# High weights against high and low moving parts: two 256-column matmuls into the same columns, in two of three pairs of retention's heads

## The chip, the cores and the metric

The kernel runs on one core of a Trainium2 chip. The metric is the device time of one execution in microseconds (us). Five engines work side by side, each with its own instruction row: TensorE (PE; PEld are its weight loads), VectorE (DVE), ScalarE (ACT), GpSimd (POOL) and SyncE (SP). They wait for one another through semaphores.

## The reference, cut to what matters

One layer of a streaming encoder on 512 frames of width 2048, in float32. The part that matters here is the large projection and retention:

```python
h = rmsnorm(x, norm_gain)
proj = h @ w_in                                  # 2048 x 13392
(aq, ak, av, az, iq, ik, iw, rq, rk, rv, rz, ga, gb) = jnp.split(proj, SPLIT_POINTS, axis=-1)
...
rq = rope(rq.reshape(B, L, R_HEADS, R_KEY_DIM), positions)
rk = rope(rk.reshape(B, L, R_HEADS, R_KEY_DIM), positions) * (R_KEY_DIM ** -0.5)
b_out = retention_mixer(rq, rk, rv, ret_gn_gain) * jax.nn.silu(rz)
merged = jax.nn.sigmoid(ga) * (a_out @ w_a_out) + jax.nn.sigmoid(gb) * (b_out @ w_b_out)
```

Eight retention heads need a query and a key block of 128 channels each; the gates `ga` and `gb` have 16 blocks each.

## The kernel before

**Precision by parts.** A float32 product is made of float16 parts. A weight block is split into `wh` (high, cast by ACT at L257) and `wl` (the rest, by DVE at L143), the moving operand likewise. Three of the four part products are kept: `wh` times high, `wh` times low and `wl` times high.

**Pairs of blocks.** `gemm_pair` (L361) computes two output blocks of 128 channels for 512 frames at once from seven products instead of eight (Strassen-Winograd form). Its moving operands (`hs`, `ha` in the profile) are sums of quarters of the normed input; each has 256 columns of high parts and 256 of low parts side by side, `LO` and `HI`. A product is a run of 8 matmuls of `wh` with all 512 columns (L435) and a run of 8 of `wl` with the 256 high columns. So after it a PSUM bank's left half holds high terms and its right half the `wh` times low terms, and the two halves are still to be added. Four banks `v`, `p`, `q`, `r` serve the seven products, in the order v, p, q, r, p, v, p; some products are added onto what a bank holds already.

**Taking out.** After certain products ACT copies a bank to SBUF (`copy`, L371: tiles `pv` and `e`). `out` (L375) takes the sum or difference of a bank and such a copy into `e_t`, 512 wide, and `done` (L1484) adds the two halves of `e_t` into a quarter of the output tile `go`. Each pair does this four times: after the third product from `q`, after the sixth from `v`, and after the seventh from `p` and then from `r`. When a 512-column output has both its quarters, `finish` follows: for gates ACT's sigmoid (L1493) and a store, for retention's pair the rotation (L1174 on ACT, L1179 to L1181 on DVE).

**Weights.** Raw blocks come by SP's queue; some are summed with another block by POOL's accumulating DMA (L221) once the first `wl` of them is made, some by DVE (L268). `wh` and `wl` have three slots each. `e`, `pv` and `e_t` are among the tiles that share 28 slots (`U`).

**Order.** Instructions stand in each engine's row as the code is called; nothing reorders them. Work beside the matmuls is put off by a count of steps (`later(n, f)`), and a step is counted in `gemm_pair` after every two values of `k`, so each deferred instruction falls at a set place among TensorE's matmuls.

**The place.** The stage from 248 to 720 us runs eight heads. Each has three pairs: retention's query and key (`u_r[h]`, whose `finish` starts that head's retention) and two gate pairs (`u_g[2h]`, `u_g[2h+1]`). Retention's own steps (splits, scores, states, norm) are spread over the following two pairs and the next head's first. Rounds of a top-k (L1074, L1077) stand among them on DVE. The next stages run four `rz` pairs and eight attention pairs in the same way. Late in the kernel two stages run `gemm_pair` with `turned`, in which a `wh` already takes high and low parts as two matmuls of 256 columns into the same columns, for some of its products.

A second, general program of the same block follows in the code for inputs that the float16 one can't serve; it is not run here.

Of the kernel before, what the change touches and what calls it, by code (L numbers as in the profile page):

```python
# [16 lines left out]
AF = mybir.ActivationFunctionType  # L17
# [20 lines left out]
class General:  # L38


    fast = False
# [7 lines left out]
class Fast:  # L49


    fast = True
    dt = F16
    w = 2.0 ** 13
    x = 2.0 ** 4
# [17 lines left out]
def block_kernel(tc, flag, cfg, xT, pT, posb, posq, w_in, w_v, w_r0, w_r1, w_ik, w_a, w_b, w_o, w_ple, w_gate,  # L73
                 w_gt, w_pt, fgb, tab, gains, cst, dec, out, out_a, out_b):
    nc = tc.nc
    pe, dve, act, pool, sp = nc.tensor, nc.vector, nc.scalar, nc.gpsimd, nc.sync

    fast = cfg.fast
    un_x, un_a, un_m, un_r, un_p = (1.0 / (cfg.w * v) for v in (cfg.x, cfg.a, cfg.m, cfg.r, cfg.p))

    with contextlib.ExitStack() as ctx:
# [11 lines left out]
        def U(name, dt=F32):  # L93
            return up.tile([128, L], dt, name=name, tag="u")
# [250 lines left out]
        ALL = slice(0, L)  # L345
# [5 lines left out]
        LO, HI = slice(0, 256), slice(256, 512)  # L351
# [6 lines left out]
        SPLIT_AT = {0: 3, 2: 4, 3: 4, 4: 5, 7: 6, 8: 7, 10: 8, 12: 9}  # L358
        LOAD_AT = (0, 2, 4, 6, 8, 10, 12)

        def gemm_pair(ids, X, done, late=False, turned=False, nk=8, more=None):  # L361

            p, v, q, r = (P("ps_" + n) for n in ("p", "v", "q", "r"))
            E = {}

            def copy(n, src):
                E[n] = U(n)  # L370
                act.activation(E[n], src, AF.Copy)  # L371

            def out(f, x, y, i, c):
                t = U("e_t")
                f(t, x, y)  # L375
                done(t[:, LO], t[:, HI], i, c)

            def minus_both(t, x, y):
                dve.scalar_tensor_tensor(t, x, -1.0, y, op0=OP.mult, op1=OP.subtract)

            add, sub = dve.tensor_add, dve.tensor_sub
            f_q, f_pv, f_r = (add, minus_both, sub) if turned else (sub, sub, add)

            def last():
                copy("e3", p)
                out(f_pv, p, E["pv"], 1, HI)
                out(f_r, r, E["e3"], 1, LO)

            def first():
                if turned:  # L390
                    E["e1"] = U("e1")
                    act.activation(E["e1"][:, LO], p[:, LO], AF.Copy)
                else:
                    copy("e1", p)

            def second():
                if turned:
                    done(q[:, LO], E["e1"][:, LO], 0, LO)
                else:
                    out(f_q, q, E["e1"], 0, LO)  # L400

            after = {
                0: lambda: copy("pv", v),
                1: first,
                2: second,
                4: lambda: copy("e2", p),
                5: lambda: out(f_q, v, E["e2"], 0, HI),
                6: last,
            }
            banks = (v, p, q, r, p, v, p)  # L410
            runs = [(n, part, range(nk)) for n, part in RUNS]
            early = 4
            if late:
                runs[0:early] = [(n, part, ks) for ks in (range(7), (7,)) for n, part, _ in runs[0:early]]
            ended = [0] * 7
            count = 0
            for at, (n, part, ks) in enumerate(runs):
                at = max(at - early, 0) if late else at
                i, o = ids[n], banks[n]
                if more is not None:  # L420
                    more(at)
                elif at in SPLIT_AT and not (late and at == 2):
                    split_to(ids[0] + SPLIT_AT[at], (1 if state["turn"] else 5) if at == 2 else 1)
                if at in LOAD_AT and more is None:
                    load_to(ids[LOAD_AT.index(at)] + AHEAD + LOADS)
                if waiting and state["banks"] and 4 <= at <= 9:
                    bias_banks(waiting.popleft())
                w, c = loaded[i][part], (ALL, LO)[part]
                begin = ended[n] == 0
                for k in ks:  # L430
                    ended[n] += 1
                    x = X[PRODUCTS[n]][k]
                    moving = [(LO, v) for v in x[:2 - part]] if turned and isinstance(x, tuple) else [(c, x[:, c])]
                    for j, (co, src) in enumerate(moving):
                        pe.matmul(o[:, co], w[:, k], src, start=(n < 4 and begin and k == 0 and j == 0),  # L435
                                  stop=(ended[n] == 2 * nk), skip_group_check=True)
                    count += 1
                    if count % (16 // nk) == 0:
                        step()
                if ended[n] == 2 * nk and n in after:  # L440
                    after[n]()
# [168 lines left out]
        u_r, u_g = [], []  # L610
        for h in range(NH):
            u_r.append(block_pair(col(RQ, h), col(RK, h)))
            for n in (2 * h, 2 * h + 1):
                g, m = ((GB, 2 * n), (GA, 2 * n - 16))[n >= 8]
# [9 lines left out]
        for n in range(1, 16):  # L624
            for at in NARROW_AT if fast else ():
                if at // 8 == n - 1:
                    for _, f in list(to_make)[:LOOK]:
                        f[0]()
                    m, f = to_make.popleft()
# [42 lines left out]
        cs = cp.tile([128, 130], F32, name="cs")  # L672
# [313 lines left out]
        Xh, h_step = combos(lambda k: xn[k], lambda k: xn[k + 8], "h", lambda n, k: x_at.get((n, k)))  # L986
# [99 lines left out]
        for r in range(16):  # L1086
            for t in range(1, NT):
                f = lambda r=r, t=t: topk_round(t, r == 15)
# [382 lines left out]
            if late_rounds:  # L1471
                late_rounds.popleft()()

        def gate_pair(ids, finish):
            if state["banks"]:
                for n in ROUNDS_AT:
                    later(n, late_round)
            t = B("go")
            outs = [t[:, 0:512], t[:, 512:1024]]
            have = [0, 0]  # L1480

            def done(c0, c1, i, q):
                o = outs[i]
                dve.tensor_add(o[:, q], c0, c1)  # L1484
                have[i] += 1
                if have[i] == 2:
                    later(1, lambda: finish(i, o))

            gemm_pair(ids, Xh, done)

        def to(dst, func):
            def finish(i, o):
                act.activation(o, o, func, scale=un_x)  # L1493
                later(2 if fast else 0, lambda: act.dma_start(dst[i], o))
            return finish
# [5 lines left out]
        for h in range(NH):  # L1501
            if fast and h == NH - 1:
                state["rate"] = BG_RATES[3]
            if state["rate"] == BG_RATES[2]:
                later(38, lambda: hold(True))
                later(64, lambda: hold(False))
            if fast:
                for n in ROUNDS_IN_HEAD if h else ():
                    later(n, late_round)
            gate_pair(u_r[h], retention(h))  # L1510
            for n in (2 * h, 2 * h + 1):
                d, m = ((sgb, 2 * n), (sga, 2 * n - 16))[n >= 8]
                state["turn"] = fast and n == 2 * h
                gate_pair(u_g[n], to(d[m:m + 2], AF.Sigmoid))
        state["rate"] = BG_RATES[4]
        state["banks"] = True
        for n, u in enumerate(u_rz):
            y = B("y2")
# [232 lines left out]
        for m in PAIRED:  # L1751
# [19 lines left out]
            elif m - 8 not in narrow:  # L1771
                t = B("sm")
                s, o = t[:, 0:512], t[:, 512:1024]
# [64 lines left out]
        for m in range(MF):  # L1838
            i = u_p[m // 4][0]
# [3 lines left out]
            h, l = loaded[i]  # L1843
# [324 lines left out]
        if fast:  # L2168
# [36 lines left out]
RET_SPLITS = {("k", 0): 16, ("k", 1): 21, ("q", 0): 18, ("q", 1): 24, ("v", 0): 26, ("v", 1): 37,  # L2205
              ("vd", 0): 40, ("vd", 1): 45}
KEYS_AT = 30, 31
ROUNDS_AT = 19, 44
ROUNDS_IN_HEAD = 15, 44, 106, 106
QK_LOW = 5, 9  # L2210
# [105 lines left out]
```

## Time and profile before

| | us |
|---|---|
| median of 3 runs | 1551.54 (1551.16 to 1551.79) |
| the profiled execution | 1552.11 |
| its span, first to last instruction | 1550.3 |
| retention's heads in it | 248.4 to 720 |

The granted clock of TensorE is 0.998 of full speed over the span. In the profile's rows the first number is the start in us from the span's start, the second the duration; a row such as `ps_r<-hs,wh 128*128 128x512 f16 x8` is eight matmuls into bank `ps_r` with `hs` moving and `wh` loaded, 512 columns each. What stands in brackets is the idle time just before, and what ended it. Matmuls are pipelined: a run's modelled end lies later than the next run's possible start. Rows of groups give durations in ns as least, median and greatest.

### The profile page before, as it was taken

Reading aid. Unit: us, or ns where it says so; the run is one execution under the profiler, and the core shown is the slowest. Engines: PE = TensorE matmul, PEld = TensorE weight load, DVE = VectorE, ACT = ScalarE, POOL = GpSimd, SP = SyncE. Lnnn points to the kernel's source line nnn. Section 1 sums busy time; section 2 is a strip of 40 time slices with the busy share of each in tenths; the row PEclk is TensorE's granted clock in tenths of the full one; section 3 lists DMA queues with packets and bytes.
Section 4 is the critical chain, followed back from the end, with each engine's and each line's share of the span. In section 5 each row is a group of like instructions: output and inputs, shape, how many; then the busy total and the mean of one; then the engine's idle time right before and its main releaser. Section 6 shows DMA issues by size and latency. Waiting matters only on the chain.

```text
span 1550.3 us, 26188 instructions
## 1 busy us (share of the span) xinstructions
PE 1532.5 (99%) x9537; PEld 896.5 (58%) x9537; DVE 1357.5 (88%) x2776; ACT 978.1 (63%) x1491; POOL 224.4 (14%) x261
## 2 busy tenths in 40 slices
PE   9999999999999999999999999999999999999997
PEld 5654445666656656556555665655555556647765
DVE  8899889999999999998788888788879999998975
ACT  7565545665665665687877776577633555576654
POOL 3000121111111111112441121200000111101101
PEclk9999999999999999999999999999999999999999
DMA  8436989899898899789999999999666899878974
GB/s 323 133 120 204 259 215 248 217 226 233 211 229 230 207 231 232 205 221 258 287 251 242 225 249 232 262 357 345 208 211 190 204 224 234 236 225 233 264 213 148
DMA packets 136269, 358.15 MB, mean 231 GB/s; under 512 B 22209, under 2 KB 34753, under 8 KB 136129
## 3 DMA queue, kind: packets, MB, share of 16 engines
q1 hardware_dynamic: 94368, 230.08, 43.8%
q0 software_dynamic: 28656, 101.20, 34.9%
q10 hardware_dynamic: 13104, 25.09, 4.4%
q8 instruction: 76, 1.25, 0.3%
q14 instruction: 65, 0.52, 0.1%
HBM read 311.76 MB, written 42.99 MB: 229 GB/s over the span
## 4 chain that ended last, share of the span: by engine, by line
PE 65%; DVE 20%; ACT 7%; issue 4%; DMA 3%; ACTq 0%; SPq 0%; DVEq 0%
PE ps_p L435 18%; PE ps_v L435 12%; PE ps_r L435 6%; DVE wl L143 6%; PE ps_q L435 5%; DVE e_t L375 3%; ACT wh L257 2%; PE ps_vn L1142 2%; PE ps_vn L1144 2%; PE ps_vn L1143 2%; PE ps_iq L337 1%; PE ps_iq L339 1%; PE ps_iq L338 1%; DVE go L1484 1%; DVE wraw L268 1%
## 5 line engine op out<-in xcount | busy, mean ns | idle before, releaser
L143 DVE SCALAR_TENSOR_TENSOR wl<-wraw,wh 128x1024 f16<-128x1024 f32 (+3 forms) x461 | 557.0, 1220 | 90.6 <-ACT wh L257 89.4
L257 ACT ACTIVATE wh<-wraw 128x1024 f16<-128x1024 f32 (+3 forms) x484 | 489.2, 1024 | 131.7 <-DVE wraw L268 75.9
L435 PEld LDWEIGHTS <-wh 128*128 128x128 f16 x3224 | 313.5, 98 | 317.9 <-ACT wh L257 9.9
L435 PEld LDWEIGHTS <-wl 128*128 128x128 f16 x2968 | 287.8, 98 | 72.8 <-DVE wl L143 9.6
L221 POOL DMA_DIRECT2D wraw<-w_in x120 | 106.6, 972 | 564.4 <-DVE wl L143 482.2
L435 PE MATMUL ps_p<-hs,wh 128*128 128x512 f16 x640 | 152.5, 379 | 0.0
L371 ACT ACTIVATE e<-ps_p 128x512 f32<-128x512 f32 x158 | 93.0, 589 | 51.3 <-PE ps_p L435 42.0
L435 PE MATMUL ps_p<-hs,wl 128*128 128x256 f16 x640 | 84.4, 273 | 1.6 <-ACT rq L1190 1.1
L435 PE MATMUL ps_r<-hs,wh 128*128 128x512 f16 x320 | 75.7, 379 | 2.5 <-ACT wh L257 2.2
L435 PE MATMUL ps_q<-ha,wh 128*128 128x512 f16 x320 | 75.7, 379 | 0.0
L435 PE MATMUL ps_v<-ha,wh 128*128 128x512 f16 x320 | 75.6, 379 | 0.0
L435 PE MATMUL ps_v<-hs,wh 128*128 128x512 f16 x320 | 75.6, 379 | 0.0
L435 PE MATMUL ps_p<-ha,wh 128*128 128x512 f16 x320 | 75.6, 379 | 0.0
L1493 ACT ACTIVATE go<-go 128x512 f32<-128x512 f32 x40 | 25.2, 630 | 79.1 <-DVE go L1484 79.1
L1484 DVE TENSOR_TENSOR go<-e_t 128x256 f32<-128x256 f32 x160 | 68.0, 425 | 5.8
L1037 ACT ACTIVATE mk<-relf,thr 128x512 f16<-128x512 f32 (+3 forms) x128 | 67.5, 553 | 1.3 <-ACT go L1493 1.2
L268 DVE TENSOR_TENSOR wraw<-wraw 128x1024 f32<-128x1024 f32 x53 | 64.9, 1225 | 1.8
L339 PEld LDWEIGHTS <-wl 128*128 128x128 f16 x396 | 38.8, 98 | 40.2 <-DVE wl L143 0.2
L337 PEld LDWEIGHTS <-wh 128*128 128x128 f16 x396 | 38.9, 98 | 37.0 <-DVE z L150 0.3
L338 PEld LDWEIGHTS <-wh 128*128 128x128 f16 x396 | 38.8, 98 | 36.5
L221 POOL DMA_DIRECT2D wraw<-w_o x24 | 21.1, 932 | 235.7 <-DVE wl L143 101.3
L339 PE MATMUL ps_w<-bh,wl 128*128 128x512 f16 x128 | 48.5, 379 | 0.0
(467 smaller groups left out, 2885.3 us busy)
## 6 DMA issues: line engine op xcount, KB each, us to landing
wraw<-w_in SPq DMA_DIRECT2D x170, 512.0 KB, 5.6
wraw<-w_in POOLq DMA_DIRECT2D x120, 512.0 KB, 8.1
wraw<-w_o SPq DMA_DIRECT2D x32, 512.0 KB, 5.6
wraw<-w_o POOLq DMA_DIRECT2D x24, 512.0 KB, 7.6
wraw<-w_gate SPq DMA_DIRECT2D x24, 512.0 KB, 5.3
wraw<-w_v SPq DMA_DIRECT2D x16, 512.0 KB, 7.7
wraw<-w_b SPq DMA_DIRECT2D x16, 512.0 KB, 6.5
wraw<-w_gate POOLq DMA_DIRECT2D x15, 512.0 KB, 7.2
```

What stands on the lines that cost most here:

```text
L143: dve.scalar_tensor_tensor(l, src, 1.0 if gain is None else gain, h, op0=OP.mult, op1=OP.subtract, **({"accum_out": column()} if checked a ...
L221: pool.dma_start(out=view(raw_tiles[r], nk, cols), in_=src[:, k0:k0 + nk, :], accum_op=OP.add)
L257: act.activation(h, raw, AF.Copy, scale=cfg.w)
L268: dve.tensor_add(raw, raw, view(raw_tiles[plus], nk, cols))
L337: pe.matmul(o, h[:, k, w], a, start=(s == order[0]), stop=False)
L338: pe.matmul(o, h[:, k, w], b, start=False, stop=False)
L339: pe.matmul(o, l[:, k, w], a, start=False, stop=(s == order[-1]))
L371: act.activation(E[n], src, AF.Copy)
L375: f(t, x, y)
L435: pe.matmul(o[:, co], w[:, k], src, start=(n < 4 and begin and k == 0 and j == 0), stop=(ended[n] == 2 * nk), skip_group_check=True)
L1037: act.activation(bias_e[b][i // per][:, ln * (i % per):ln * (i % per + 1)], relf[:, :ln], AF.Sign, bias=thr[:, q:q + 1])
L1484: dve.tensor_add(o[:, q], c0, c1)
```

## The change

`gemm_pair` gets an argument `compact`. With it each `wh` takes two matmuls of 256 columns, with the high and with the low part, both into the bank's left half. The halves need no adding later, so `copy` copies 256 columns, and `out` passes its function to `done`, which writes the sum or difference of bank and copy straight into the quarter of `go`. The table `COMPACT` sets it for retention's pair and the second gate pair of every head, in the float16 program alone. The first gate pair and all later stages stay as they were.

```diff
-        def gemm_pair(ids, X, done, late=False, turned=False, nk=8, more=None):
+        def gemm_pair(ids, X, done, late=False, turned=False, nk=8, more=None, compact=False):
...
                 E[n] = U(n)
-                act.activation(E[n], src, AF.Copy)
+                cs = LO if compact else ALL
+                act.activation(E[n][:, cs], src[:, cs], AF.Copy)
 
             def out(f, x, y, i, c):
+                if compact:
+                    return done(x[:, LO], y[:, LO], i, c, f)
                 t = U("e_t")
                 f(t, x, y)
                 done(t[:, LO], t[:, HI], i, c)
...
-                    moving = [(LO, v) for v in x[:2 - part]] if turned and isinstance(x, tuple) else [(c, x[:, c])]
+                    if turned and isinstance(x, tuple):
+                        moving = [(LO, v) for v in x[:2 - part]]
+                    elif compact:
+                        moving = [(LO, x[:, v]) for v in (LO, HI)[:2 - part]]
+                    else:
+                        moving = [(c, x[:, c])]
                     for j, (co, src) in enumerate(moving):
                         pe.matmul(o[:, co], w[:, k], src, start=(n < 4 and begin and k == 0 and j == 0),
                                   stop=(ended[n] == 2 * nk), skip_group_check=True)
...
-        def gate_pair(ids, finish):
+        def gate_pair(ids, finish, compact=False):
...
-            def done(c0, c1, i, q):
+            def done(c0, c1, i, q, f=dve.tensor_add):
                 o = outs[i]
-                dve.tensor_add(o[:, q], c0, c1)
+                f(o[:, q], c0, c1)
...
-            gemm_pair(ids, Xh, done)
+            gemm_pair(ids, Xh, done, compact=compact and fast)
...
-            gate_pair(u_r[h], retention(h))
+            gate_pair(u_r[h], retention(h), COMPACT[0])
...
-                gate_pair(u_g[n], to(d[m:m + 2], AF.Sigmoid))
+                gate_pair(u_g[n], to(d[m:m + 2], AF.Sigmoid), COMPACT[1 + n % 2])
...
+COMPACT = True, False, True
```

No instruction changes its place relative to the others. DVE at the end of head 1's second gate pair, whose sums fall into the first matmuls of head 2 (`e_t` the 512-wide sum, `go` the output, `gst` to `grs` and `y` the norm of the head before), before:

```order
L1296 TENSOR_SCALAR grs<-gmv 128x4
L375 TENSOR_TENSOR e_t<-ps_v,e_3872 128x512
L1484 TENSOR_TENSOR go<-e_t 128x256
L143 SCALAR_TENSOR_TENSOR wl,stats<-wraw,wh 128x1024
L375 TENSOR_TENSOR e_t<-ps_p,pv 128x512
L1484 TENSOR_TENSOR go<-e_t 128x256
L375 TENSOR_TENSOR e_t<-ps_r,e_3937 128x512
L1484 TENSOR_TENSOR go<-e_t 128x256
L143 SCALAR_TENSOR_TENSOR wl,stats<-wraw,wh 128x1024
```

The same place with the change:

```order
L1304 TENSOR_SCALAR grs<-gmv 128x4
L1492 TENSOR_TENSOR go<-ps_v,e_4054 128x256
L143 SCALAR_TENSOR_TENSOR wl,stats<-wraw,wh 128x1024
L1492 TENSOR_TENSOR go<-ps_p,pv 128x256
L1492 TENSOR_TENSOR go<-ps_r,e_4133 128x256
L143 SCALAR_TENSOR_TENSOR wl,stats<-wraw,wh 128x1024
```

Three of the four places of a pair stand here; at each, two rows became one of half the width, and what follows moved up. TensorE at the start of retention's first pair, the first weights of the first product, before:

```order
L435 MATMUL ps_v<-hs_1551,wh 128x512
L435 LDWEIGHTS wh
L435 MATMUL ps_v<-hs_1617,wh 128x512
L435 LDWEIGHTS wh
L435 MATMUL ps_v<-hs_1704,wh 128x512
```

With the change:

```order
L443 MATMUL ps_v<-hs_1551,wh 128x256
L443 LDWEIGHTS wh
L443 MATMUL ps_v<-hs_1551,wh 128x256
L443 LDWEIGHTS wh
L443 MATMUL ps_v<-hs_1617,wh 128x256
```

Each matmul of high weights became two of half the columns, and the weights are loaded again between them.

## The prediction

> **What bounds the kernel now.** I read the page first, then the three stages around the change by busy time, then TensorE's own rows, then the DVE and ACT rows ahead of its gaps.
>
> ```profile
> PE 1532.5 (99%) x9537; PEld 896.5 (58%) x9537; DVE 1357.5 (88%) x2776; ACT 978.1 (63%) x1491; POOL 224.4 (14%) x261
> PE 65%; DVE 20%; ACT 7%; issue 4%; DMA 3%; ACTq 0%; SPq 0%; DVEq 0%
> ```
>
> TensorE is busy all the time, yet the chain that ended last lies on DVE for a fifth of the span: somewhere TensorE runs close behind DVE. Three stretches follow: retention's eight heads, the stage of the next gate pairs, and the attention queries and keys (columns: span, then busy us of PE, PEld, DVE, ACT, POOL with instruction counts, granted clock, DMA share, GB/s).
>
> ```profile
> 248.40:720.00 471.60, 466.26 (x3070) 282.74 (x3072) 439.19 (x895) 300.62 (x416) 75.16 (x84) 1.00 0.88 224
> 720.00:800.00 80.00, 79.86 (x547) 46.40 (x539) 64.54 (x114) 67.21 (x99) 31.41 (x36) 1.00 0.98 265
> 800.00:950.00 150.00, 150.00 (x998) 90.28 (x996) 126.88 (x243) 111.65 (x183) 29.93 (x40) 1.00 0.94 243
> ```
>
> In the heads DVE is busy 439.2 of 471.6 us, 93%, and TensorE shows 5.3 us of idle time. From 800 to 950 us the same kind of pairs runs with DVE at 84.6% and TensorE shows none. In the heads TensorE's matmul line sat idle for these (us, times):
>
> ```profile
>   ACT wh L257: 10.8, 20
>   DVE wl L143: 10.4, 23
>   ACT rq L1190: 1.1, 3
> ```
>
> All three are split operands that ACT and DVE make in turn. These idle times partly lie beside matmuls still in flight, so I size the gaps from the start times. Head 2 (its three pairs begin at 363.5, 382.2 and 401 us) and the worst place of head 7:
>
> ```profile
> 368.70 1.89 PE L435 MATMUL ps_q<-ha,wh 128*128 128x512 f16 x8
> 370.90 1.90 PE L435 MATMUL ps_r<-hs,wh 128*128 128x512 f16 x8 [0.31 <-ACT wh L257]
> ...
> 391.71 1.04 PE L435 MATMUL ps_r<-hs,wl 128*128 128x256 f16 x8
> 393.01 1.05 PE L435 MATMUL ps_p<-hs,wl 128*128 128x256 f16 x8 [0.26 <-ACT rq L1190]
> 393.89 1.89 PE L435 MATMUL ps_p<-hs,wh 128*128 128x512 f16 x8
> 395.62 1.89 PE L435 MATMUL ps_v<-ha,wh 128*128 128x512 f16 x8
> 397.70 0.39 PE L435 MATMUL ps_v<-ha,wl 128*128 128x256 f16 x2 [0.19 <-DVE wl L143]
> ...
> 659.76 1.89 PE L435 MATMUL ps_q<-ha,wh 128*128 128x512 f16 x8
> 662.52 1.68 PE L435 MATMUL ps_r<-hs,wh 128*128 128x512 f16 x7 [0.87 <-ACT wh L257]
> ```
>
> An undisturbed run of eight wide matmuls lets the next one start after 1.73 us (393.89 to 395.62); eight narrow ones take 0.87. So 370.90 is 0.47 late, 393.01 is 0.43, 397.70 is 0.35, and 662.52 is 1.03 late. The same subtraction for every run of the stage finds 28 late places, 9.6 us together: 3.0 ahead of `ps_r<-hs,wh` in retention's own pair, 2.5 ahead of `ps_p<-hs,wl` and 2.8 ahead of `ps_v<-ha,wl` in the first gate pair, 1.0 ahead of `ps_r<-hs,wh` in the second, 0.3 elsewhere. The stage row agrees: a run shows 1.89 where its successor can start at 1.73, so each gap hides 0.16, and 5.3 + 28 x 0.16 = 9.8 us. Call the budget 9.6. No gain in this stage can be larger than about 10 us.
>
> **What stands ahead of a gap.** DVE, then ACT, before 370.90:
>
> ```profile
> 363.48 0.68 DVE L375 TENSOR_TENSOR e_t<-ps_v,e 128x512 f32<-128x512 f32 x1
> 364.20 0.43 DVE L1484 TENSOR_TENSOR go<-e_t 128x256 f32<-128x256 f32 x1
> 366.46 0.69 DVE L375 TENSOR_TENSOR e_t<-ps_p,pv 128x512 f32<-128x512 f32 x1 [0.69 <-ACT e L371]
> 367.18 0.42 DVE L1484 TENSOR_TENSOR go<-e_t 128x256 f32<-128x256 f32 x1
> 367.52 0.68 DVE L375 TENSOR_TENSOR e_t<-ps_r,e 128x512 f32<-128x512 f32 x1
> 368.24 0.43 DVE L1484 TENSOR_TENSOR go<-e_t 128x256 f32<-128x256 f32 x1
> 368.70 0.63 ACT L1493 ACTIVATE go<-go 128x512 f32<-128x512 f32 x1 [1.34 <-DVE go L1484]
> 369.79 1.06 ACT L257 ACTIVATE wh<-wraw 128x1024 f16<-128x1024 f32 x1 [0.46 <-ACT go L1493]
> ```
>
> The weights that TensorE waits for are cast by ACT at 369.79, behind a sigmoid that waits for the last sum of the previous pair on DVE. That pair is a second gate pair, one of those changed.
>
> **The change, part by part.**
>
> Removed on DVE and ACT. Each pair takes out its products four times; each time a 512-wide sum into `e_t` and a 256-wide sum of its halves become one 256-wide sum from PSUM, and the copies `pv`, `e1`, `e2`, `e3` become 256 wide.
>
> ```profile
> L375 DVE TENSOR_TENSOR e_t<-ps_v,e x55: 672/684/692, 265.1 to 1487.8; 128x512 f32<-128x512 f32 x55
> L1484 DVE TENSOR_TENSOR go<-e_t x160: 424/425/427, 260.0 to 1021.8; 128x256 f32<-128x256 f32 x160
> L1935 DVE TENSOR_TENSOR go<-ps_q,e x5: 417/417/425, 1407.9 to 1481.3; 128x256 f32<-128x256 f32 x5
> L371 ACT ACTIVATE e<-ps_p x158: 572/591/613, 254.7 to 1489.6; 128x512 f32<-128x512 f32 x158
> L392 ACT ACTIVATE e<-ps_p x7: 378/384/385, 1148.0 to 1476.6; 128x256 f32<-128x256 f32 x7
> ```
>
> L1935 and L392 are the new forms, already in the trace. DVE saves 4 x (0.684 + 0.425 - 0.417) = 2.8 us a pair, 44 us in 16 pairs; ACT saves 4 x (0.591 - 0.384) = 0.8 us a pair, 13 us in all. None of it is span by itself; it counts only where a gap ends sooner. DVE's share in the heads falls from 93 to (439.2 - 44) / 464 = 85%, the share at which the 800 us stage shows no gap.
>
> Gap by gap. Before 370.90 the three fused sums save about 0.7 us each, and the shorter `e3` copy 0.2: 2.3 us sooner, against 0.47 late. It cannot be sooner than the chain from TensorE allows: the pair's last run ends near 363.5 + 0.16, then copy 0.38, two sums 0.8, sigmoid 0.63, its store's issue 0.4, cast 1.06, so 367.0, well before 370.43. In the first gate pair DVE's rows run without a break from the sums of retention's pair, which is changed, through the rotation to both late `wl`; these sums lie ahead of 393.01 and 397.70 alike. I expect 1.1 to 2 us sooner there (bounded by the copies that wait for TensorE), against 0.43 and 0.35. The second gate pair inherits that, against 0.35 at most. Head 7's 1.03 has the same chain with one mask more on ACT; 2.3 us covers it. The four places under 0.12 us I did not follow; they make 0.4. Bounds: 0 to 9.8 us; I take 9.2.
>
> What hides the sooner work: DVE writes its `wl` into three slots and ACT its `wh` into three, so both can run ahead of TensorE by that much only. Where the relief is more than the gap, it turns into idle DVE time, and this is where 44 us of DVE become 9 us of span.
>
> Slots. `e_t` took one of 28 shared slots each time; 64 claims fall away, and the waits for a slot's last readers pass to other tiles. Before, they show in the heads as
>
> ```profile
> ACT e L371 <- DMA wraw<-w_in: 1.6, 3, 0.5
> ```
>
> at most: three waits of the copies. With fewer claims a slot comes round later, so I cost the move at nothing; were three such waits new and on the path, they would be 1.6 us.
>
> Loads. The sooner a `wl` ends, the sooner POOL adds the next block to the raw weights; nothing is moved on POOL's or SP's queue.
>
> ```profile
> 380.79 0.86 POOL L221 DMA_DIRECT2D wraw<-w_in x1 [12.75 <-DVE wl L143]
> DMA to landing us min/median/max: 7.2/7.9/11.0
> 389.89 1.06 ACT L257 ACTIVATE wh<-wraw 128x1024 f16<-128x1024 f32 x1
> ```
>
> The add of 380.79 lands by the median at 388.7, 1.2 us ahead of the cast that needs it, which moves sooner too. So I cost it at nothing, but this cover is thin: a landing at the maximum, 391.8, would make `ps_p<-hs,wl` about 1.4 us late.
>
> Added on TensorE. Each matmul of high weights becomes two of 256 columns, each with its own weight load: 16 pairs x 7 products x 8 = 896 more of both. The last stage has the very form (16 narrow matmuls, two for each block of high weights, into the same 256 columns):
>
> ```profile
> 1399.85 1.91 PE L435 MATMUL ps_p<-rh,wh 128*128 128x256 f16 x16
> 1401.59 1.04 PE L435 MATMUL ps_v<-rs,wl 128*128 128x256 f16 x8
> ...
> 1409.43 1.89 PE L435 MATMUL ps_p<-rs,wh 128*128 128x512 f16 x8
> 1411.16 1.91 PE L435 MATMUL ps_v<-rh,wh 128*128 128x256 f16 x16
> 1412.91 1.04 PE L435 MATMUL ps_v<-rh,wl 128*128 128x256 f16 x8
> L435 PEld LDWEIGHTS <-wh x3224: 95/98/99, 248.4 to 1489.0; 128*128 128x128 f16 x190
> ```
>
> Sixteen narrow take 1.74 and 1.75 us where eight wide take 1.73: 0.018 a run, times 112 runs, 2.0 us, and all of it on the path. By the rows' rounding it is 0.6 to 2.8. A load takes 98 ns and a narrow matmul streams for 109, so it stays covered, by 11 ns. The Trainium skill (TensorE: Matmul & The Clock Gate, Back-to-back issue gap) gives an isolated matmul N / 2.4 GHz + 2.5 ns; by that the estimate would be 896 x 2.5 ns = 2.2 us, and the sum 0.2 us later.
>
> The sum against the profiled execution: its time is 1552.11 us (span 1550.3 and 1.8 around it). 1552.1 - 9.2 + 2.0 = 1544.9. The median of the three runs, 1551.54, is 0.57 below it, so I forecast 1544.4 us.
>
> **Rivals.**
>
> Half of it comes back as other waits: the cast's wait for the added weights' landing, copies that wait for TensorE, or the unchanged first gate pair with its retention work. For it: the thin 1.2 us above, and a DMA share of 0.88 in the stage. Against it: each gap needs only 0.3 to 0.5 us. Recovering about 5 us gives 1551.5 - 5 + 2.0 = 1548.5.
>
> The gaps stay whole: what TensorE waits for is late for a reason other than DVE's queue, as a fixed distance from an earlier matmul would be. For it: the gap before `ps_v<-ha,wl` is 0.35 in nearly every head. Against it: behind 393.01 that wait is spaced by DVE's own unbroken row, not by a matmul. Then only the cost is left: 1551.5 + 2.0 = 1553.5, no measurable change.
>
> Slower: the added weight loads are not covered. Place: each second narrow matmul. For it: the cover is only 11 ns. Against it: the quoted runs of sixteen. Above 9.2 us / 896 = 10 ns each the change loses, above 14 ns measurably; wholly exposed, 98 ns x 896 = 88 us, it ends near 1551.5 + 88 - 9.2 = 1630. The Trainium skill speaks for this side in the section named: it puts a sustained stream of load and matmul at about 131 ns for N = 512 and 81 for N = 128. By that two halves would cost at least 2 x 81 - 131 = 31 ns more, 28 us in 896, and the kernel would end near 1570 as an estimate. The trace disagrees: 216 ns for 512 columns (1.73 / 8) and 109 for 256.
>
> **How the numbers follow.** The forecast case, at least 7.1 us of the gaps gone (own range 1542.4 to 1546.4), has 0.66. Half back has 0.20, gaps whole 0.07, slower 0.04, and 0.03 is for more than I can account for. The low end takes the full 9.8 us against the least cost, 1551.5 - 9.8 + 0.6 = 1542.3; the high end, 1549.4, reaches over the half case and leaves out its worst part (0.05), the whole gaps, the loss and the surplus, 0.19 together. A measurement here tells about 0.2%, 3.1 us. Faster than that: 0.66 + 0.03 + just over half of the half case, 0.80; within it: the rest of that case and the whole gaps, 0.16; slower: 0.04.
>
> **What the changed kernel's profile would show.** The matmul line's waits for `wh` and `wl` in the heads fall from 20 and 23 to a few; `ps_r<-hs,wh` follows `ps_q<-ha,wh` without a gap; runs of sixteen take 1.74 to 1.75 us; DVE is busy near 85% of the stage with more idle time, put down to ACT; the 720 to 1030 us stretch looks as before, some 7 us sooner. I am wrong if runs of sixteen take more than 1.83 us (then 896 loads cost 11 us), or if late places remain with a DMA landing as releaser.

## The result, and the profile after

| | before | changed |
|---|---|---|
| median of 5 runs each, one beside the other | 1551.79 us (1551.16 to 1552.17) | 1543.44 us (1543.34 to 1543.97) |
| the profiled execution | 1552.11 | 1543.44 |
| its span | 1550.3 | 1541.6 |

The ratio is 0.9946, with a 95% interval of 0.9934 to 0.9959: 8.35 us less by the medians, 8.7 by the spans. The forecast was 1544.4.

The page of the changed kernel, busy time and then the chain that ended last by engine:

```profile
PE 1529.4 (99%) x10433; PEld 986.7 (64%) x10433; DVE 1317.6 (85%) x2712; ACT 970.0 (63%) x1491; POOL 225.0 (15%) x261
PE 88%; DVE 6%; ACT 2%; issue 1%; DMA 1%; SPq 0%; DVEq 0%; ACTq 0%
```

The chain has moved to TensorE: 65% of the span before, 88% now, and DVE's share of it fell from 20% to 6%. TensorE's busy time can't show this, since it read 99% both times. The same three stretches as before, moved with the work (span, then busy us of PE, PEld, DVE, ACT, POOL with counts, granted clock, DMA share, GB/s):

```profile
248.40:711.60 463.20, 463.20 (x3954) 372.52 (x3952) 401.13 (x837) 293.64 (x418) 75.00 (x84) 1.00 0.90 228
712.00:792.00 80.00, 80.00 (x555) 46.78 (x547) 62.68 (x109) 65.98 (x98) 31.72 (x37) 1.00 0.96 262
792.00:942.00 150.00, 150.00 (x998) 90.32 (x997) 126.72 (x243) 111.29 (x183) 29.51 (x40) 1.00 0.93 245
```

In the heads TensorE has no idle time left, with 884 matmuls more in the row (896 by the change; the row before also takes in the first 12 of the next stage). DVE's 401.1 us are 87% of the stretch, near the 85% forecast, but only 38 us less than before where 44 were forecast; weight loads rose from 282.7 to 372.5 us, 80% of it. The next two stretches are as they were.

TensorE around the place where head 2 stood 0.47 us late, and the end of the stage:

```profile
361.28 1.91 PE L443 MATMUL ps_p<-hs,wh 128*128 128x256 f16 x16
363.03 1.91 PE L443 MATMUL ps_v<-hs,wh 128*128 128x256 f16 x16
...
367.40 1.04 PE L443 MATMUL ps_p<-ha,wl 128*128 128x256 f16 x8
368.27 1.91 PE L443 MATMUL ps_q<-ha,wh 128*128 128x256 f16 x16
370.02 1.91 PE L443 MATMUL ps_r<-hs,wh 128*128 128x256 f16 x16
...
711.67 1.05 PE L1058 MATMUL ps_bias<-mk,d 128*32 128x512 f16 x16
```

`ps_r<-hs,wh` follows `ps_q<-ha,wh` after 1.75 us, as any run of sixteen does. The first `ps_bias` behind the heads began at 719.39 before: 7.7 us sooner. I repeated the subtraction of starts for the whole stage: 29 late places of 9.75 us before (the prediction's 28, and 0.1 at that `ps_bias`), and now only the 0.09 us at the `ps_bias`.

DVE, then ACT, ahead of that place:

```profile
362.23 0.42 DVE L1492 TENSOR_TENSOR go<-ps_v,e 128x256 f32<-128x256 f32 x1
362.57 1.22 DVE L143 SCALAR_TENSOR_TENSOR wl<-wraw,wh 128x1024 f16<-128x1024 f32 x1
...
364.13 0.42 DVE L1492 TENSOR_TENSOR go<-ps_p,pv 128x256 f32<-128x256 f32 x1 [0.34 <-ACT e L372]
364.48 0.42 DVE L1492 TENSOR_TENSOR go<-ps_r,e 128x256 f32<-128x256 f32 x1
...
362.68 0.63 ACT L1501 ACTIVATE go<-go 128x512 f32<-128x512 f32 x1 [1.89 <-DVE go L1492]
363.72 0.38 ACT L372 ACTIVATE e<-ps_p 128x256 f32<-128x256 f32 x1 [0.40 <-ACT go L1501]
...
364.94 0.62 ACT L1501 ACTIVATE go<-go 128x512 f32<-128x512 f32 x1
366.02 1.06 ACT L257 ACTIVATE wh<-wraw 128x1024 f16<-128x1024 f32 x1 [0.46 <-ACT go L1501]
```

The cast that TensorE waited for ends at 367.08 and is needed at 370.02, 2.9 us ahead; before, it ended at 370.85 for a start due at 370.43. Against TensorE it comes 3.4 us sooner, where 2.3 were worked out. The waits of the stage (engine and tile that waits, what it waits for, us in all, times, longest), before:

```profile
ACT go L1493 <- DVE go L1484: 67.5, 32, 3.2
DVE wl L143 <- ACT wh L257: 14.8, 26, 0.9
ACT e L371 <- PE ps_v L435: 2.5, 5, 0.5
```

and changed:

```profile
ACT go L1501 <- DVE go L1492: 39.7, 24, 1.9
DVE wl L143 <- ACT wh L257: 39.5, 60, 1.8
ACT e L372 <- PE ps_p L443: 41.5, 49, 1.9
```

ACT's sigmoid waits 28 us less for DVE's last sums, and DVE waits 25 us more for ACT's casts. ACT's copies (`e` and `pv` together) wait 46.5 us for TensorE, where they waited 3.0 before. The two engines had been passing one chain back and forth ahead of TensorE; now both have slack in it, and the chain starts when TensorE's products are ready.

### The profile page after: what moved, and what is told of

The parts are those of the page before. It is cut to its first block, busy times and chain, and to the rows that moved or that the text cites. A ratio compares the mean times of both kernels' runs of the same rounds, so it can differ in the third digit from the quotient of the medians.

```text
span 1541.6 us, 27918 instructions
## 1 busy us (share of the span) xinstructions
PE 1529.4 (99%) x10433; PEld 986.7 (64%) x10433; DVE 1317.6 (85%) x2712; ACT 970.0 (63%) x1491; POOL 225.0 (15%) x261
## 4 chain that ended last, share of the span: by engine, by line
PE 88%; DVE 6%; ACT 2%; issue 1%; DMA 1%; SPq 0%; DVEq 0%; ACTq 0%
PE ps_p L443 27%; PE ps_v L443 18%; PE ps_q L443 9%; PE ps_r L443 9%; PE ps_vn L1151 2%; PE ps_vn L1150 2%; PE ps_vn L1152 2%; PE ps_iq L339 1%; PE ps_iq L337 1%; PE ps_iq L338 1%; DVE wl L143 1%; ACT bm L1610 1%; PE ps_pg L2018 1%; PE ps_pg L2019 1%; PE ps_pg L2020 1%
## 5 line engine op out<-in xcount | busy, mean ns | idle before, releaser
L443 PEld LDWEIGHTS <-wh 128*128 128x128 f16 x4120 | 402.2, 98 | 239.0 <-issue 1.5
L443 PE MATMUL ps_p<-hs,wh 128*128 128x256 f16 (+1 forms) x896 | 153.2, 318 | 0.0
L372 ACT ACTIVATE e<-ps_p 128x512 f32<-128x512 f32 (+1 forms) x158 | 83.3, 527 | 91.7 <-PE ps_p L443 85.1
L443 PE MATMUL ps_q<-ha,wh 128*128 128x256 f16 (+1 forms) x448 | 76.0, 318 | 0.0
L443 PE MATMUL ps_r<-hs,wh 128*128 128x256 f16 (+1 forms) x448 | 75.9, 318 | 0.0
L443 PE MATMUL ps_v<-ha,wh 128*128 128x256 f16 (+1 forms) x448 | 75.9, 318 | 0.0
L443 PE MATMUL ps_p<-ha,wh 128*128 128x256 f16 (+1 forms) x448 | 75.9, 318 | 0.0
L443 PE MATMUL ps_v<-hs,wh 128*128 128x256 f16 (+1 forms) x448 | 75.9, 318 | 0.0
L337 PEld LDWEIGHTS <-wh 128*128 128x128 f16 x396 | 38.9, 98 | 36.6
L338 PEld LDWEIGHTS <-wh 128*128 128x128 f16 x396 | 38.8, 98 | 36.6
L338 PE MATMUL ps_w<-bh,wh 128*128 128x512 f16 x128 | 48.5, 379 | 0.0
```

The costliest lines, as they stand in the source:

```text
L337: pe.matmul(o, h[:, k, w], a, start=(s == order[0]), stop=False)
L338: pe.matmul(o, h[:, k, w], b, start=False, stop=False)
L372: act.activation(E[n][:, cs], src[:, cs], AF.Copy)
```

## The experiments

Times are medians; each kernel ran beside the kernel before on the same chip. "Gaps" is the sum of the late starts over 0.06 us in TensorE's row, from the first head to the first `ps_bias`; it is 9.75 us before.

| kernel | us | before, same chip | ratio (95%) | gaps, us | first `ps_bias` |
|---|---|---|---|---|---|
| changed | 1543.44 | 1551.79 | 0.9946 (0.9934 to 0.9959) | 0.1 | 711.67 |
| all | 1544.38 | 1551.94 | 0.9952 (0.9938 to 0.9965) | 0.1 | 712.84 |
| ret_only | 1543.75 | 1551.94 | 0.9948 (0.9934 to 0.9961) | 0.4 | 711.23 |
| second_only | 1545.5 | 1551.94 | 0.9956 (0.9943 to 0.997) | 2.6 | 713.67 |
| first_only | 1544.48 | 1551.94 | 0.9954 (0.9941 to 0.9968) | 2.1 | 712.48 |
| dve_back | 1545.47 | 1551.68 | 0.9959 (0.9946 to 0.9973) | 1.3 | 713.23 |
| act_back | 1543.38 | 1551.68 | 0.9947 (0.9933 to 0.9961) | 0.1 | 711.27 |
| no_cost | 1541.58 | 1551.68 | 0.9934 (0.992 to 0.9948) | 0.1 | 709.18 |
| dve_more | 1555.94 | 1551.68 | 1.0026 (1.0016 to 1.0037) | 13.3 | 723.07 |
| dve_first | 1547.91 | 1552.32 | 0.9972 (0.996 to 0.9983) | 3.9 | 716.12 |
| dve_first_act | 1554.91 | 1552.32 | 1.0017 (1.0008 to 1.0026) | 11.6 | 723.71 |
| alternate | 1548.16 | 1552.01 | 0.9974 (0.9965 to 0.9983) | 4.9 | 714.83 |
| also_qk | 1544.06 | 1552.01 | 0.9949 (0.9935 to 0.9962) | 0.1 | 712.34 |

**Which pair.** Four kernels set the table of pairs differently; the order is retention's pair, first gate pair, second gate pair.

```diff
-COMPACT = True, False, True
+COMPACT = True, True, True      # all
+COMPACT = True, False, False    # ret_only
+COMPACT = False, False, True    # second_only
+COMPACT = False, True, False    # first_only
```

> All three pairs of a head in the narrow form. Theory (DVE's row: the shorter sums end the waits, and none is left with two pairs): only the cost is added, 8 pairs x 7 runs x 0.020 us = 1.1 us, so about 1544.6 us against 1543.4 with two pairs and 1551.6 before. Rival (the gain grows with the DVE time saved): 2.8 us of DVE a pair more, so clearly faster than 1543.

> Only retention's pair in the narrow form. Theory: its relief runs on in DVE's unbroken row through the first gate pair into the second and closes 5.3 and 1.0 us of gaps; then DVE waits for ACT's casts (three breaks of 0.45 to 0.85 us in the second gate pair before), the relief is lost, and the 3.3 us ahead of ps_r in the next head's first pair stay. 6.3 - 1.1 = 5.2 us gain, about 1546.4. Rival (a pair's sums help only the gap directly behind them): 4.2 us gain, 1547.4. Rival (each pair has an equal share): half of 9.9, less 1.1: 1547.7.

> Only the second gate pair in the narrow form. Theory: its sums lie ahead of ps_r in the next head's first pair (3.3 us of gaps), and DVE's row from there to the first gate pair's late wl has breaks of only 0.2 us, so the relief carries on and closes the other 6.3 us as well: 9.6 - 1.1 = 8.5 us gain, about 1543.1, as fast as two pairs or a little faster. Rival (help only directly behind): 3.3 - 1.1 = 2.2 us gain, 1549.4. Rival (equal shares): 1547.7.

> Only the first gate pair in the narrow form. Theory: of its sums one lies ahead of the 2.8 us before ps_v<-ha,wl, and three ahead of the 1.0 us in the second gate pair; behind these DVE waits for ACT's casts and the relief is lost, so 3.3 ahead of ps_r in retention's pair and 2.5 ahead of ps_p<-hs,wl stay: 3.8 - 1.1 = 2.7 us gain, about 1548.9. Rival (equal shares): 1547.7.

`all` came out as expected: nothing is left to gain, and eight more pairs cost 1.12 us from the first matmul of the heads to the first `ps_bias` (464.21 us against 463.09), which is 8 x 7 = 56 runs at 0.020. The other three came at none of the times expected: `ret_only` at 1543.75 for 1546.4, `first_only` at 1544.48 for 1548.9, and `second_only` at 1545.5 for 1543.1, the other way. A single pair per head, whichever it is, recovers 7.2 to 9.3 of the 9.75 us: 0.4 are left with retention's pair, 2.6 with the second gate pair (1.9 of them ahead of `ps_v<-ha,wl`), 2.1 with the first (1.5 in `ps_p`). So a gap isn't tied to the pair just ahead of it, and the two changed pairs don't share the gain: the gain needs 9.75 / 8 = 1.2 us per head, and each pair alone saves DVE 2.8 and ACT 0.8.

**Which engine.** `dve_back` gives DVE its old time back, but behind the fused sum, so that the result leaves early and DVE is busy as long as before; `act_back` gives ACT its 512-wide copies back.

```diff
                 if compact:
-                    return done(x[:, LO], y[:, LO], i, c, f)
+                    done(x[:, LO], y[:, LO], i, c, f)
+                    for _ in range(2):
+                        dve.tensor_add(y[:, HI], R["ct"][:, LO], R["st"][:, LO])
+                    return
```

> The change, and behind each fused sum two 256-column sums of constants on DVE (0.34 us apart each, so 0.69 us, about what the fusing saved), written into the unused half of the copy, so that no further slot is taken. ACT's shorter copies stay. Theory (any DVE time taken off a head ends the gaps, wherever it is taken): the gaps come back, less what the shorter copies give; 7 to 10 us of gaps and the 2 us of cost, 1551 to 1553.5 us. Rival (the shorter copies on ACT end them): 1543.4 to 1545. Rival (the 64 slots no longer taken): 1543.4.

```diff
-                cs = LO if compact else ALL
-                act.activation(E[n][:, cs], src[:, cs], AF.Copy)
+                if compact:
+                    act.activation(E[n].rearrange("p (j c) -> p j c", j=2),
+                                   src[:, None, LO].to_broadcast([128, 2, 256]), AF.Copy)
+                else:
+                    act.activation(E[n], src, AF.Copy)
```

> The change with ACT's copies 512 columns wide again (the left half copied twice). Theory: DVE alone matters, gaps under 1 us, 1543.4 to 1544.3. Rival (ACT's 0.8 us a pair end the gaps): back towards 1552.

`act_back` did what was expected, nothing: with the sums fused, the copies' length has no effect. `dve_back` did not: 1545.47 lies outside all three expectations, nearest to that of ACT's shorter copies. The same 430 us in each kernel (columns as above), in the order before, changed, `dve_back`, `act_back`:

```profile
270.00:700.00 430.00, 424.66 (x2798) 258.04 (x2797) 402.21 (x819) 274.14 (x380) 66.40 (x74) 1.00 0.88 222
```

```profile
270.00:700.00 430.00, 430.00 (x3677) 345.79 (x3676) 372.30 (x773) 272.14 (x387) 66.27 (x74) 1.00 0.90 228
```

```profile
270.00:700.00 430.00, 429.52 (x3661) 343.90 (x3660) 409.39 (x886) 268.29 (x386) 66.26 (x74) 1.00 0.90 227
```

```profile
270.00:700.00 430.00, 430.00 (x3680) 346.03 (x3679) 371.54 (x773) 283.36 (x387) 66.27 (x74) 1.00 0.90 228
```

In `dve_back` DVE is busy 409.4 us, 95%, more than the 402.2 of before, and yet TensorE's idle time is 0.5 us and not 5.3. Over the whole heads it is 441.5 us against 438.4. So DVE's busy time alone does not make the gaps; ACT's copies are short in this kernel, and what they do is taken up below. DVE's rows at the place in head 2, DVE and then ACT, show what is different:

```profile
362.65 0.42 DVE L1495 TENSOR_TENSOR go<-ps_v,e 128x256 f32<-128x256 f32 x1
362.99 0.88 DVE L378 TENSOR_TENSOR e<-ct,st 128x256 f32<-128x256 f32 x2
...
366.06 0.42 DVE L1495 TENSOR_TENSOR go<-ps_r,e 128x256 f32<-128x256 f32 x1
...
363.11 0.63 ACT L1504 ACTIVATE go<-go 128x512 f32<-128x512 f32 x1 [2.07 <-DVE go L1495]
364.14 0.38 ACT L372 ACTIVATE e<-ps_p 128x256 f32<-128x256 f32 x1 [0.40 <-ACT go L1504]
...
367.59 1.06 ACT L257 ACTIVATE wh<-wraw 128x1024 f16<-128x1024 f32 x1 [0.46 <-ACT go L1504]
```

The sum from `ps_v` leaves DVE at 363.07 and ACT's sigmoid starts at once, while DVE still works off the added sums. Those lie beside ACT's work instead of ahead of it.

**The cost alone, and more load.** `no_cost` keeps the wide matmuls and sums and copies only the left halves, so that the products of high weights with low parts are missing from its output; `dve_more` adds one 512-wide sum to every head of the kernel before.

```diff
-                    elif compact:
-                        moving = [(LO, x[:, v]) for v in (LO, HI)[:2 - part]]
```

> The sums and copies of the change with the wide matmuls of before; the products of high weights with low parts, in the right half, are left out of the output. Theory: as changed without its cost on TensorE, 2.0 us sooner, 1541.4. Rival (narrow matmuls cost nothing, or themselves help): 1543.4 or later.

```diff
+                    if extra:                # second(), retention's pair only
+                        dve.tensor_add(E["e1"], R["ct"], R["st"])
```

> Before, with one more 512-column sum of constants on DVE in each head (0.61 to 0.69 us a head, 5 to 5.5 us in eight). Theory (DVE's work of a head, with its waits for ACT, is what sets the head's period of 58.06 us): nearly all of it comes out as time, 4.5 to 5.5 us, about 1556.5 to 1557.5. Rival (each gap has its own local cause): a sum in one place delays at most the wait behind it and the rest absorbs it, under 2.5 us, below 1554.5.

`no_cost` ends 1.86 us below the changed kernel, as the cost term said. `dve_more` is 4.3 us slower than before for 8 x 0.68 = 5.5 us of DVE time, 0.78 us for one: a little under the range expected, and well over the 2.5 us of the rival. Its added sum stands behind a result as well, the sum from `q`, but right ahead of the `wl` of the same pair. In head 2 that `wl` ends at 380.18, and `ps_p<-hs,wl` starts at 380.25, 0.26 us late; seven heads have this new late place. So where the chain has no slack, DVE time behind one result is ahead of the next and costs most of its length; in `dve_back`, where the sums are short and leave early, it costs little.

**Ahead of the result, then ACT as well.** `dve_first` puts the added time ahead of the fused sum; `dve_first_act` has `act_back`'s copies besides, so that only the narrow matmuls and the freed `e_t` slots are left of the change. DVE is as busy over the heads as before in both: 442.4 and 442.2 us.

```diff
                 if compact:
+                    for _ in range(2):
+                        f(y[:, HI], x[:, LO], y[:, LO])
                     return done(x[:, LO], y[:, LO], i, c, f)
```

> The change, and ahead of each fused sum the same sum twice more into the unused half of the copy (0.34 us apart each), so that DVE's time and the moment at which the output leaves DVE are both as before; ACT's copies stay short, no slot is taken. The two sums behind instead of ahead left 1.2 us of gaps in the heads at the same DVE time. New theory (what closes the gaps is that each sum's result leaves DVE 0.7 us sooner, for ACT's sigmoids, swaps and casts that stand behind it, not DVE's time): 6 to 9 us of gaps and the 2 us of cost, 1549.5 to 1553. Rival (ACT's shorter copies): few gaps, 1543.4 to 1546. Rival (the slots): 1543.4 to 1546.

> As the run before it, and ACT's copies 512 columns wide again: of the change only the narrow matmuls and the 64 slots are left. New theory: all gaps are back, 9.7 us, and the cost of 2 us on TensorE comes on top, 1553 to 1554.5, slower than before. Rival (the slots no longer taken): 1543.4 to 1546.

The same 430 us in `dve_first`, then in `dve_first_act`:

```profile
270.00:700.00 430.00, 428.39 (x3632) 340.44 (x3630) 408.20 (x883) 267.29 (x385) 66.41 (x74) 1.00 0.89 224
```

```profile
270.00:700.00 430.00, 422.66 (x3556) 332.48 (x3555) 401.93 (x869) 271.63 (x376) 64.64 (x72) 1.00 0.87 221
```

`dve_first` has the DVE load of `dve_back` and 3.9 us of gaps instead of 1.3: the place of the time matters, but 3.9 is well under the 9.75 of before, and the time is below the range expected. It is also above both rivals. With the short ACT copies gone as well the gaps are back, 11.6 us; so with DVE's time back ahead of the sums the copies hold the rest, and the slots account for none of the gain. One place holds 1.5 of the 1.9 us by which 11.6 exceeds the 9.75 of before (ACT, DVE, then TensorE in `dve_first_act`):

```profile
614.41 2.01 ACT L257 ACTIVATE wh<-wraw 128x1024 f16<-128x1024 f32 x2 [1.52 <-DMA wraw<-w_in]
615.50 1.23 DVE L143 SCALAR_TENSOR_TENSOR wl<-wraw,wh 128x1024 f16<-128x1024 f32 x1 [1.19 <-ACT wh L257]
...
629.42 1.05 PE L447 MATMUL ps_p<-hs,wl 128*128 128x256 f16 x8 [1.58 <-ACT rq L1202]
```

A cast waits for raw weights, DVE's row stands behind it, and `ps_p<-hs,wl` is 1.74 us late where the kernel before has 0.29. (The bracket names `rq`, whose end lies near; the `wl` that is loaded ends on DVE at 629.35.) The place in head 2 of `dve_first_act`, DVE, ACT, then TensorE:

```profile
364.35 0.88 DVE L379 TENSOR_TENSOR e<-ps_v,e 128x256 f32<-128x256 f32 x2
365.14 0.41 DVE L1496 TENSOR_TENSOR go<-ps_v,e 128x256 f32<-128x256 f32 x1
...
367.25 0.88 DVE L379 TENSOR_TENSOR pv<-ps_p,pv 128x256 f32<-128x256 f32 x2 [0.56 <-ACT e L372]
...
369.17 0.41 DVE L1496 TENSOR_TENSOR go<-ps_r,e 128x256 f32<-128x256 f32 x1
...
365.59 0.63 ACT L1505 ACTIVATE go<-go 128x512 f32<-128x512 f32 x1 [3.28 <-DVE go L1496]
366.62 0.60 ACT L372 ACTIVATE e<-ps_p 128x512 f32<-128x512 f32 x1 [0.40 <-PE ps_v L447]
...
370.71 1.06 ACT L257 ACTIVATE wh<-wraw 128x1024 f16<-128x1024 f32 x1 [0.46 <-ACT go L1505]
...
369.62 1.91 PE L447 MATMUL ps_q<-ha,wh 128*128 128x256 f16 x16
371.82 1.38 PE L447 MATMUL ps_r<-hs,wh 128*128 128x256 f16 x11 [0.29 <-ACT wh L257]
```

The chain can be read here link by link: a sum on DVE (to 365.55), ACT's sigmoid (365.59), ACT's copy (366.62), DVE's sums from `p` and `r` (367.25 to 369.58), the second sigmoid (369.62 on ACT), the cast (370.71 to 371.77), and TensorE 0.45 us late at 371.82.

Four kernels make a square of gaps: DVE's time back ahead of the results and copies long 11.6, the same and copies short 3.9; only the fused sums and copies long 0.1 (`act_back`), both as in the change 0.1. Short copies are worth 7.7 us in the one row (1.5 of them at 629.42) and nothing in the other. The parts don't add, since they shorten one chain that needs only so much. In this square the results leave DVE later and DVE has more to do, both at once. Only `dve_back` parts the two: at the same DVE time, 1.3 us of gaps with the added sums behind the results against 3.9 with them ahead. That is with short copies; the same with long ones was not run. The slack in the chain goes against the gaps: ACT's copies wait 46.5 us for TensorE in the changed kernel, 34.6 in `act_back`, 13.8 in `dve_back`, 7.2 in `dve_first`, 4.1 in `dve_first_act` and 3.0 before.

**Does the relief last?** `alternate` makes only retention's pair narrow, and only in heads 0, 2, 4 and 6; `also_qk` adds the eight attention pairs of the later stage, which had no gaps.

```diff
-            gate_pair(u_r[h], retention(h), COMPACT[0])
+            gate_pair(u_r[h], retention(h), h % 2 == 0)
...
-COMPACT = True, False, True
+COMPACT = True, False, False
```

> Only retention's pair of every second head (0, 2, 4, 6) in the narrow form: 28 runs of sixteen, 0.5 us of cost. With that pair in all heads 0.3 us of gaps were left. Theory (DVE's and ACT's work of the heads is one chain that runs 1.2 us a head longer than TensorE's, and what is taken off it is kept until it is used up): 2.8 us on DVE and 0.8 on ACT in every second head cover about two heads' 2.4 us, so 1 to 2.5 us of gaps are left, 1543.2 to 1545. Rival (what is taken off helps within its own head alone): half of the gaps, 4.9 us, are left, 1547.2.

```diff
-            gate_pair(u_qk[h], qk_out)
+            gate_pair(u_qk[h], qk_out, True)
```

> The change, and the eight attention pairs after the heads in the narrow form too. There TensorE shows no gap before. Theory (the narrow matmuls cost 0.020 us a run wherever there is no gap to close): 56 runs, 1.1 us more than the change, 1544.5. Rival (DVE time saved is time saved): earlier than 1543.4.

`alternate` keeps 4.9 us of gaps, as the rival said and not the theory; its time is 1 us above the rival's 1547.2. Its rows of TensorE with an idle time between 370 and 490 us:

```profile
370.36 1.92 PE L443 MATMUL ps_r<-hs,wh 128*128 128x256 f16 x16 [0.25 <-ACT wh L257]
...
453.87 0.39 PE L443 MATMUL ps_v<-ha,wl 128*128 128x256 f16 x2 [0.19 <-DVE wl L143]
...
465.81 1.90 PE L443 MATMUL ps_r<-hs,wh 128*128 128x512 f16 x8 [0.19 <-ACT wh L257]
485.66 1.92 PE L443 MATMUL ps_r<-hs,wh 128*128 128x256 f16 x16 [0.25 <-ACT wh L257]
```

All lie in head 3 or in the first products of heads 2 and 4, ahead of anything the narrow pair could give. Of the 9.75 us before, 5.2 lay in the odd heads and the first products behind them and 4.5 in the even heads and the first products behind those; 4.5 and 0.4 us are left. The 0.4 is the first `ps_r<-hs,wh` of head 7 (657.97), behind a narrow pair in head 6; it was 1.03. A head with a narrow pair loses nearly all of its own gaps and hands on little.

`also_qk` came out as expected. Its stage and the next stage's first `ps_w` (least, median, greatest ns, first and last start), `also_qk` and then the changed kernel:

```profile
792.00:942.00 150.00, 150.00 (x1419) 131.41 (x1418) 107.13 (x210) 107.53 (x181) 29.82 (x40) 1.00 0.91 244
...
L337 PE MATMUL ps_w<-bh,wh x128: 377/379/379, 1009.4 to 1125.0; 128*128 128x512 f16 x128
```

```profile
L337 PE MATMUL ps_w<-bh,wh x128: 377/379/379, 1007.6 to 1123.2; 128*128 128x512 f16 x128
```

DVE fell from 126.7 to 107.1 us in that stage, and the stage became longer: from the first `ps_bias` to the first `ps_w` it takes 297.0 us against 295.9, 1.12 us more, or 56 runs at 0.020. Relief where TensorE never waits is only cost.

No kernel with all its products is measurably better than the changed one. `ret_only` has half its cost and 0.3 us more of gaps; the two can't be told apart here.

## Why the prediction was right, and where its reason was not

- **The place.** Right: 7.7 of the 8.7 us of span are gained in retention's heads, from the gaps that the subtraction of starts had found. The stage behind gained 0.4 us, most of it where one more late `ps_p<-hs,wl` is gone (744.97 before).
- **The gaps, 9.2 of 9.6.** A little low: 9.66 are gone in the heads, and 0.3 us more in starts that differ by less than 0.06 us. Less the 2.2 us of cost this is the 7.7 us by which the first `ps_bias` comes sooner. Behind the heads 0.4 us is gained as told, and 0.6 between 1109 and 1122 us, 0.4 of it at a wait ahead of `ps_o<-pt` (1121.70 before) that I had not followed. In the other kernels this wait is 0.07 to 0.48 us long and does not go with the gaps (0.48 in `alternate`, 0.11 in `dve_first_act`), so this part is luck. The forecast counts from 1551.54 us and the kernel before ran at 1551.79 beside the changed one: the gain forecast was 7.1 us and the medians give 8.35, so the sum was 1.2 us low and the time 0.96.
- **The cost, 2.0 us.** Right: 112 runs at 1.7466 against 1.7270 us are 2.2 us by the trace. From the first matmul of the heads to the first `ps_bias` the changed kernel takes 463.09 us and `no_cost` 460.85, 2.24 less; the medians give 1.86. `all` and `also_qk` cost 0.020 a run against the 0.018 taken.
- **The loss by uncovered loads.** It did not come: the 256 columns here take 1.7466 / 16 = 109 ns in the changed pairs of all eight heads, and 512 take 216. The Trainium skill (TensorE: Matmul & The Clock Gate, Back-to-back issue gap) expects 81 ns for a sustained load and matmul at N = 128 and 131 ns at N = 512, which the trace contradicts; its figure for one matmul by itself, N / 2.4 GHz + 2.5 ns, fits both. The cover of 11 ns that the prediction read off a load of 98 ns was not the limit either. In retention's own steps of the kernel before, 128-column matmuls with a load of 98 ns each start 56 ns apart, so these loads overlap:

```profile
397.93 0.83 PE L1199 MATMUL ps_rs<-rq,rk 128*128 128x128 f16 x12
L1199 PEld LDWEIGHTS <-rk x96: 97/98/98, 282.0 to 690.8; 128*128 128x128 f16 x96
```

- **Half back, by the added weights' landing or by copies.** It did not come. TensorE's matmul line in the heads has nothing left that it sat idle for, and no cast of the changed kernel's heads waits for raw weights. The copies do wait for TensorE, 46.5 us, but TensorE does not wait for them. The slots, costed at nothing, are settled by `dve_first_act`.
- **Gaps whole.** The distance of 0.35 us ahead of `ps_v<-ha,wl` went with the rest; it was DVE's row.
- **The reason.** Two readings stand in the prediction. "What stands ahead of a gap", with the working gap by gap, was right: a chain that crosses from DVE to ACT several times per head and was 1.2 us per head longer than TensorE's work. The other, by shares, does not hold: it takes DVE's fall from 93 to 85% as support, since the 800 us stage shows no gap at that share, but `dve_back` has DVE at 95% and still gains 6.2 us. The split of the 2.3 us at 370.90, 0.7 for each sum and 0.2 for the shorter copy, doesn't carry over to the stage either. The fused sums end the gaps by themselves (`act_back`), and with DVE's time put back ahead of them the short copies still end 7.7 us. It is shown that the fused sums, or one pair of three, take off all or most, and that the shares can't be added. The Trainium skill (Perfetto Trace Analysis, Identifying the Most-Contended Engine) takes the engine with the highest occupancy as the one to work on first, with other measures for TensorE; shortening DVE's rows did pay here, but from before to `dve_back` DVE's occupancy rose from 402.2 to 409.4 of 430 us and the time fell.
- **The expectation of locality.** After the result I first expected `ret_only` at 1546.4 and `first_only` at 1548.9, from which gap stands behind which pair. They came at 1543.75 and 1544.48. `second_only` I expected at 1543.1, with its relief carried on to every gap; it came at 1545.5, with 1.9 us left ahead of the next head's `ps_v<-ha,wl`. Relief in any one pair reaches most of the gaps within about a head's length, and then it is used up.

Open: why so little passes to the next head, which nothing here isolates; what `dve_back` would leave with long copies, so how much of the gain at full-length copies is that the results come sooner and how much that DVE has less to do; whether the casts in `dve_back`, which wait 2.4 us for raw weights in five places (none before), make part of its 1.3 us of gaps; and what sets the wait at 1121.70.

## What to carry to other kernels

Size a gain from the late starts of the engine that bounds the kernel, place by place, and take that sum as the ceiling for that stage; a busy share of 93% on another engine says neither that this engine is the cause nor what relief would bring. Where two engines hand work back and forth, find the chain, and ask of each saving whether it lies ahead of a result that is waited for: time given back behind the result lost 2.1 us of the 8.35 here, and the same time ahead of it 3.9, both with short copies and each against its own run of before. Once the chain fits under the bounding engine's work the rest of the relief is worth nothing, and what it costs on the bounding engine (here 0.020 us a run) stays.

## What was not expected of the hardware

Loading the same weights twice for two halves of the columns cost 0.020 us per eight, 2.5 ns for each added load and matmul, with a load of 98 ns beside a matmul of 109. It held in the changed kernel over the 463 us of the heads, in which the loads were busy 80% of the time, and in `all`, where they were busy 90% (416.4 of 464.3 us). The price is near the forecast; that it does not hang on 11 ns of cover, as the 56 ns from load to load above show, was not expected.
